# The width-31 convolution accumulates in PSUM instead of SBUF, and two sets of modulation sums start five projections later

## The chip, the cores and the metric

The kernel runs on one core of one Trainium2 chip. The metric is the device time of one execution in microseconds (us); 1197.08 us is the median of three runs of the kernel before (1196.81 to 1198.6). Engines are named as in the profile: PE is TensorE, DVE is VectorE, ACT is ScalarE, POOL is GpSimd, SP issues the transfers.

## The reference

One layer of a diffusion backbone on 1024 latent tokens of width 1024, with 256 context tokens. All data are fp32.

```python
mx = split(silu(c) @ w_ada + b_ada, 6)          # shift, scale, gate of the mixer; the same of the FFN
h  = rms_norm(x, g0) * (1 + mx[1]) + mx[0]
a, gl, q, k, v, o, gates = split(h @ w_in)      # 512 columns each, 16 gate columns
u  = a * sigmoid(gl)
u  = dwconv(u, conv_w, conv_b)                  # 31 taps along each grid row of 64 tokens, per channel
u  = silu(layer_norm(u))
hm = mlstm_bidirectional(q, k, v, gates)        # 4 heads of 128, both directions, start state from the context
m  = sigmoid(o) * head_norm(hm)
x  = x + mx[2] * rms_norm(concat(u, m) @ w_out, g1)
h2 = rms_norm(x, g2) * (1 + mx[4]) + mx[3]
x  = x + mx[5] * rms_norm(conv_ffn(h2), g3)     # up projection, 3-tap convolution, SiLU gate, down projection
```

## The kernel before

Channels lie on the 128 partitions and tokens on the free axis. Every fp32 matmul of a projection is three passes on split operands (a high part and a rest), so each weight block of 128 columns is loaded into a `raw` buffer (three of them), copied to the high part by ACT, and subtracted to the rest by POOL or DVE (line 134).

The order of the first half is this. After the norm of x and its modulation come the first two GLU blocks (column blocks j = 0, 1 of `a` and `gl`) and then j = 2, 3; `glu_evac` (line 274, DVE) writes the product `u[j]`. Then follow the V and gate columns (`vpass(1)`, with the preparation of the context in the middle of it, then `vpass(0)`, with the gate arithmetic `gates()` woven in), and twelve projections in the order k0, q0, k1, k2, k3, q1, q2, q3, o0 to o3 (`proj`, line 679). Into the projections the mLSTM heads are woven: head 0 from the third weave on, then `conv_norm` (the LayerNorm of the convolution), then heads 1 to 3. The output projection (lines 951 to 953) and the FFN follow.

`conv(j)` is the convolution of one block of 128 channels: ACT writes the centre tap and the bias into `accf[:, j]` in SBUF (line 278), and thirty SCALAR_TENSOR_TENSOR instructions on DVE (line 286) add one tap each, with `u[j]` and `accf[:, j]` as inputs, both in SBUF, and `accf[:, j]` as output. Edge taps touch fewer columns: 16 rows of 64 less the offset, so 784 to 1008 elements. All four convolutions are issued at a priority of 100000 behind everything else. A planner orders the instructions of PE, DVE, ACT and POOL at build time by priority and its own estimate of readiness, so taps go into the places where it expects DVE to be free; on the chip each engine then runs its list strictly in order. The SP queue keeps the order of the program.

PSUM has eight banks: pool `mm` with four tiles for projections, pool `tp` with four tiles for everything else (`TP()`): transposes, state updates (`upd`, line 713 on DVE), scores, and the two products of a token chunk in `mlstm_head`, `pv` and `pc`, which four DVE and ACT instructions read (lines 813 to 821).

The modulation vectors are sums over 1024 columns: `ada_step` asks for one more `raw` buffer of `w_ada` (512 KB by SP) and one SCALAR_TENSOR_TENSOR of 128x1024 with an accumulator on DVE (line 228). 32 such steps (shift and scale of the FFN norm, the two gates) are taken two at a time at the start of each of the twelve projections, and the last eight together after them, before the output projection.

Of the kernel before, what the change touches and what calls it, by code (L numbers as in the profile page):

```python
# [8 lines left out]
F32 = mybir.dt.float32  # L9
F32R = mybir.dt.float32r  # L10
AF = mybir.ActivationFunctionType
# [19 lines left out]
def hybrid_block(ctx: ExitStack, tc: tile.TileContext, x, cx, cc, small, gb, w_ada,  # L31
# [10 lines left out]
    wp = wide.enter_context(tc.tile_pool(name="wp", bufs=11, side="right"))  # L42
    rawp = wide.enter_context(tc.tile_pool(name="rawp", bufs=3, side="right"))
    mm = wide.enter_context(tc.tile_pool(name="mm", bufs=4, space=bass.MemoryType.PSUM))
    tp = wide.enter_context(tc.tile_pool(name="tp", bufs=4, space=bass.MemoryType.PSUM))
    early = ExitStack()
    t4 = early.enter_context(tc.tile_pool(name="t4", bufs=10))

# [20 lines left out]
    def wide_tile(n, per, dt=F32):  # L69

        return Cols([S8(dt).rearrange("p (k n) -> p k n", k=per) for _ in range(n // per)])
# [10 lines left out]
    def MM():  # L82
        return mm.tile([P, 512], F32, tag="mm", name="mm")

    def TP():
        return tp.tile([P, 512], F32, tag="tp", name="tp")

    def H2(n=512):
        return sm.tile([P, 512], F32, tag="h2", name="h2", bufs=8)[:, 0:n]
# [185 lines left out]

    def conv(j):
        uv = u[j].rearrange("p (r c) -> p r c", c=W)
        act.activation(out=accf[:, j], in_=u[j], func=AF.Identity, scale=conv_w[:, j, 15:16],
                       bias=conv_b[:, j:j + 1])
        for t in range(CW):  # L280
            o = t - 15
            if o == 0:
                continue
            lo, hi = max(0, -o), min(W, W - o)
            dst = accf[:, j].rearrange("p (r c) -> p r c", c=W)[:, :, lo:hi]
            dve.scalar_tensor_tensor(out=dst, in0=uv[:, :, lo + o:hi + o], scalar=conv_w[:, j, t:t + 1],  # L286
                                     in1=dst, op0=ALU.mult, op1=ALU.add)


    AB2 = const.tile([P, 2, 8], F32, name="AB2")  # L290
# [40 lines left out]
    def ada_step(n):  # L331
        for _ in range(n):
            next(ada_g, None)
# [142 lines left out]
    for j in range(2):  # L476
        u[j] = T4()
        for hf in range(2):
            glu_evac(j, hf, *ps0[j, hf])
    accf = wide_tile(4, 2)  # L480
    vw = None
    with prio(100000):
        conv(0)
# [195 lines left out]
    def proj(i, evac):  # L679
        w = ahead.pop(i)  # L680
        n = order.index(i) + 1
        if n < len(order):
            ahead[order[n]] = load_blk(order[n])
        ada_step(2)
        for hf in range(2):
            hi, lo = hT[hf]
            ps = MM()
            yield from mm_block(ps, w, hi, lo)
            evac(hf, ps)
        return w  # L690
# [53 lines left out]
    def mlstm_head(h):  # L744
# [38 lines left out]
        for g in range(2):  # L783
            hh = H2().rearrange("p (c n) -> p c n", n=P)
            s_ps = TP()
            for t in range(4):
                s = slice((4 * g + t) * P, (4 * g + t + 1) * P)
                pl.matmul(s_ps[:, t * P:(t + 1) * P], kT[h][:, s], qT[:, s], start=True, stop=True)
                yield
            for d in range(2):  # L790
                p = Dt[d][:, g * 512:(g + 1) * 512]
                dve.tensor_tensor(out=p, in0=s_ps, in1=p, op=ALU.mult)
            for t in range(4):
                if t == 2 and pend and hn is not None:
                    yield from tails()
                c = 4 * g + t
                cs = slice(c * P, (c + 1) * P)
                pv, pc = TP(), TP()
                nv = pv[:, 0:258].rearrange("p (d n) -> p d n", d=2)
                nc_ = pc[:, 0:258].rearrange("p (d n) -> p d n", d=2)  # L800
                pl.matmul(pc[:, 0:258], qT[:, cs], Cs[c // 4][:, c % 4].rearrange("p d n -> p (d n)"),
                          start=True, stop=True)
                yield
                for d in range(2):
                    pl.matmul(nv[:, d], Dt[d][:, cs], vx[h][:, c, :], start=True, stop=True)
                    yield
                gc = gcol(0, h, c)
                gs = slice(gc, gc + 63, 62)

                dn = SM(4, "dn")  # L810
                rr, rw = dn[:, 0:2], dn[:, 2:4]
                one = lambda v: v[:, :, 128:129].rearrange("p d o -> p (d o)")
                dve.tensor_tensor(out=rr, in0=one(nc_), in1=wcol[:, gs], op=ALU.mult)
                dve.tensor_tensor(out=rr, in0=one(nv), in1=rr, op=ALU.add)
                dve.scalar_tensor_tensor(out=rw, in0=rr, scalar=-1.0, in1=rr, op0=ALU.mult, op1=ALU.max)
                dve.tensor_tensor(out=rr, in0=rw, in1=thr[:, gs], op=ALU.max)
                dve.reciprocal(out=rr, in_=rr)
                dve.tensor_tensor(out=rw, in0=rr, in1=wcol[:, gs], op=ALU.mult)
                act.mul(out=hh[:, t], in_=nv[:, 0, 0:128], mul=rr[:, 0:1])
                for src, w in ((nv[:, 1], rr[:, 1:2]), (nc_[:, 0], rw[:, 0:1]), (nc_[:, 1], rw[:, 1:2])):  # L820
                    dve.scalar_tensor_tensor(out=hh[:, t], in0=src[:, 0:128], scalar=w, in1=hh[:, t],
                                             op0=ALU.mult, op1=ALU.add)
                dve.bn_stats(out=st[:, c], in_=hh[:, t])
                dve.bn_aggr(out=mv[:, c], in_=st[:, c])
            pend.append((h, g, hh, mv))
# [39 lines left out]
    uf = accf  # L865

    def conv_norm():
        for hf in range(2):
            xh = [T4().rearrange("p (t n) -> p t n", n=512) for _ in range(2)]
            mv = SM(8, "cmv").rearrange("p (t s) -> p t s", s=2)  # L870
            st = SM(24, "cst").rearrange("p (t s) -> p t s", s=6)
            for t in range(4):
                ps = TP()
                tok = slice((4 * hf + t) * P, (4 * hf + t + 1) * P)
                for j in range(4):
                    pl.transpose(ps[:, j * P:(j + 1) * P], uf[:, j, tok], ident)
                    yield
                dve.bn_stats(out=st[:, t], in_=ps)
                dve.bn_aggr(out=mv[:, t], in_=st[:, t])
                rs = SM(1, "crs")  # L880
                rsqrt_pow(rs, mv[:, t, 1:2], 1, "h")
                nb = SM(1, "cnb")
                dve.scalar_tensor_tensor(out=nb, in0=mv[:, t, 0:1], scalar=-1.0, in1=rs, op0=ALU.mult, op1=ALU.mult)
                act.activation(out=xh[t // 2][:, t % 2], in_=ps, func=AF.Identity, scale=rs, bias=nb)
            for j in range(4):
                ps = TP()
                for t in range(4):
                    pl.transpose(ps[:, t * P:(t + 1) * P], xh[t // 2][:, t % 2, j * P:(j + 1) * P], ident)
                    yield
                act.activation(out=uf[:, j, hf * 512:(hf + 1) * 512], in_=ps, func=AF.Silu,  # L890
                               scale=ln_g[:, j:j + 1], bias=ln_b[:, j:j + 1])
        conv_done.append(True)
# [639 lines left out]
```

## Time and profile before

| | |
|---|---|
| median of three runs | 1197.08 us (1196.81 to 1198.6) |
| the profiled execution, own time | 1197.89 us |
| its span, first to last instruction | 1195.8 us |
| PE busy | 1143.2 us (96%) |
| DVE busy | 932.0 us (78%) |
| ACT busy | 523.7 us (44%) |
| POOL busy | 121.3 us (10%) |
| granted clock of TensorE, mean over the span | 0.99 |

Busy time is the union of an engine's instructions. A busy PE includes matmuls that wait inside the pipeline. The mean duration of an instruction reaches from its start to its end; the next one of the same engine may start a little before that end, so a step from start to start is shorter than a duration. Times in a row are from the start of the span.

### The profile page before, as it was taken

Reading aid. Unit: us, or ns where it says so; the run is one execution under the profiler, and the core shown is the slowest. Engines: PE = TensorE matmul, PEld = TensorE weight load, DVE = VectorE, ACT = ScalarE, POOL = GpSimd, SP = SyncE. Lnnn points to the kernel's source line nnn. Section 1 sums busy time; section 2 is a strip of 40 time slices with the busy share of each in tenths; the row PEclk is TensorE's granted clock in tenths of the full one; section 3 lists DMA queues with packets and bytes.
Section 4 is the critical chain, followed back from the end, with each engine's and each line's share of the span. In section 5 each row is a group of like instructions: output and inputs, shape, how many; then the busy total and the mean of one; then the engine's idle time right before and its main releaser. Section 6 shows DMA issues by size and latency. Waiting matters only on the chain.

```text
span 1195.8 us, 14940 instructions
## 1 busy us (share of the span) xinstructions
PE 1143.2 (96%) x5463; PEld 939.5 (79%) x5463; DVE 932.0 (78%) x1702; ACT 523.7 (44%) x952; POOL 121.3 (10%) x106
## 2 busy tenths in 40 slices
PE   6899898999898999999999999999999999999997
PEld 5788787877687777887787888878888878888885
DVE  4899999999779996568966676676668685995585
ACT  6432222242485454357545344343434355454461
POOL 2634120111302210010000000000000000000000
PEclk9899899999999999999999999999999999999999
DMA  8963110442225412442324231323132159633251
GB/s 305 329 207 121 52 37 1 142 147 65 88 89 176 140 56 89 150 167 89 104 73 132 88 122 55 132 89 132 45 132 93 75 192 391 227 112 117 80 220 71
DMA packets 51823, 153.42 MB, mean 128 GB/s; under 512 B 5589, under 2 KB 5925, under 8 KB 49958
## 3 DMA queue, kind: packets, MB, share of 16 engines
q1 hardware_dynamic: 40662, 132.28, 32.0%
q10 hardware_dynamic: 11088, 20.19, 4.5%
q8 instruction: 43, 0.70, 0.2%
q14 instruction: 30, 0.25, 0.1%
HBM read 123.83 MB, written 28.61 MB: 127 GB/s over the span
## 4 chain that ended last, share of the span: by engine, by line
PE 61%; DVE 6%; ACT 1%; issue 1%; POOL 0%; DVEq 0%; POOLq 0%; ACTq 0%
PE mm L1141 8%; PE mm L1143 8%; PE mm L1142 8%; PE c L1369 3%; PE c L1371 3%; PE c L1370 3%; PE tp L1143 3%; PE tp L1142 3%; PE tp L1141 3%; PE a L1369 3%; PE a L1371 3%; PE a L1370 2%; PE mm L951 2%; PE mm L953 2%; PE mm L952 2%; PE tp L508 2%
## 5 line engine op out<-in xcount | busy, mean ns | idle before, releaser
L286 DVE SCALAR_TENSOR_TENSOR s<-t,sml,s 128x864 f32<-128x864 f32 (+14 forms) x120 | 150.5, 1295 | 0.1
L150 PE MATMUL mm<-s,w 128*128 128x512 f32 (+1 forms) x320 | 126.6, 399 | 0.0
L151 PE MATMUL mm<-s,w 128*128 128x512 f32 (+1 forms) x320 | 124.7, 393 | 0.1
L133 ACT ACTIVATE w<-raw 128x1024 fp32r<-128x1024 f32 x94 | 97.0, 1054 | 20.6 <-DMA raw<-in_w_out_dram 5.3
L1141 PE MATMUL mm<-s,w 128*128 128x512 f32 x264 | 104.9, 397 | 0.7 <-ACT h L1214 0.7
L1142 PE MATMUL mm<-s,w 128*128 128x512 f32 x264 | 104.2, 395 | 0.0
L1143 PE MATMUL mm<-s,w 128*128 128x512 f32 x264 | 104.0, 395 | 0.0
L134 DVE TENSOR_TENSOR w<-raw,w 128x1024 fp32r<-128x1024 f32 x77 | 92.3, 1222 | 1.5 <-PE mm L952 0.8
L154 PE MATMUL mm<-s,w 128*128 128x512 f32 (+1 forms) x320 | 93.2, 400 | 0.0
L141 POOL TENSOR_TENSOR r<-yw,mhalf 128x1 f32<-128x1 f32 x16 | 9.7, 608 | 690.7 <-DVE yw L140 690.7
L1141 PE MATMUL mm<-x,w 128*128 128x512 f32 x176 | 70.5, 401 | 0.7 <-ACT h L1205 0.5
L151 PEld LDWEIGHTS mm<-s,w 128*128 128x128 f32 x320 | 60.9, 190 | 11.6 <-POOL s L265 0.7
L1141 PE MATMUL tp<-s,w 128*128 128x512 f32 x176 | 69.5, 395 | 0.0
L150 PEld LDWEIGHTS mm<-s,w 128*128 128x128 f32 x320 | 61.0, 190 | 10.9
L1142 PE MATMUL tp<-s,w 128*128 128x512 f32 x176 | 69.5, 395 | 0.0
L1143 PE MATMUL tp<-s,w 128*128 128x512 f32 x176 | 69.4, 394 | 0.0
L1142 PE MATMUL mm<-x,w 128*128 128x512 f32 x176 | 69.3, 394 | 0.0
L1143 PE MATMUL mm<-x,w 128*128 128x512 f32 x176 | 69.3, 394 | 0.0
L1197 DVE TENSOR_TENSOR h<-mm,h 128x512 f32<-128x512 f32 x22 | 15.2, 692 | 66.3 <-PE mm L1143 66.3
L1271 ACT ACTIVATE s<-x 128x512 fp32r<-128x512 f32 x62 | 38.4, 628 | 64.1 <-PE a L1371 25.0
L1256 DVE TENSOR_TENSOR s<-x,s 128x512 fp32r<-128x512 f32 x62 | 42.8, 695 | 29.0 <-ACT s L1271 29.0
L154 PEld LDWEIGHTS mm<-s,w 128*128 128x128 f32 x320 | 57.0, 189 | 10.2
(311 smaller groups left out, 2916.6 us busy)
## 6 DMA issues: line engine op xcount, KB each, us to landing
raw<-in_w_up_dram SPq DMA_DIRECT2D x44, 512.0 KB, 4.5
zv<-s ACTq DMA_DIRECT2D x77, 256.0 KB, 3.4
raw<-in_w_ada_dram SPq DMA_DIRECT2D x32, 512.0 KB, 4.2
t<-in_w_ada_dram SPq DMA_DIRECT2D x28, 512.0 KB, 5.8
x<-zv SPq DMA_DIRECT2D x14, 1024.0 KB, 5.0
raw<-in_wblk_dram SPq DMA_DIRECT2D x20, 512.0 KB, 4.8
d<-in_w_down_dram SPq DMA_DIRECT2D x28, 256.0 KB, 6.8
x<-zv SPq DMA_DIRECT2D x7, 768.0 KB, 4.2
```

Of the source, the lines that this page charges most:

```text
L133: act.activation(out=hi, in_=raw, func=AF.Copy)
L134: (eng or pool).tensor_tensor(out=lo, in0=raw, in1=hi.bitcast(F32), op=ALU.subtract)
L150: pe.matmul(o, w[0][:, k], hi[:, k], start=(k == 0), stop=False)
L151: pe.matmul(o, w[0][:, k], lo[:, k], start=False, stop=False)
L154: pe.matmul(o, w[1][:, k], hi[:, k], start=False, stop=(k == KT - 1))
L286: dve.scalar_tensor_tensor(out=dst, in0=uv[:, :, lo + o:hi + o], scalar=conv_w[:, j, t:t + 1], in1=dst, op0=ALU.mult, op1=ALU.add)
L1141: pe.matmul(ps, w[0][:, s], b[0][:, k], start=(start and k == 0), stop=False, skip_group_check=True)
L1142: pe.matmul(ps, w[0][:, s], b[1][:, k], start=False, stop=False, skip_group_check=True)
L1143: pe.matmul(ps, w[1][:, s], b[0][:, k], start=False, stop=(k == 3), skip_group_check=True)
L1369: pe.matmul(ps, o[:, 0, s], o[:, 2], start=start, stop=False, skip_group_check=True)
L1370: pe.matmul(ps, o[:, 0, s], o[:, 3], start=False, stop=False, skip_group_check=True)
L1371: pe.matmul(ps, o[:, 1, s], o[:, 2], start=False, stop=stop, skip_group_check=True)
```

## The change

The four-tile pool `tp` shrinks to two tiles, and a new pool `cv` holds one tile of two banks. `conv(j)` takes that tile: DVE writes the centre tap and the bias into it (one TENSOR_SCALAR of 128x1024 in place of the ACT instruction), 29 taps read and write it in PSUM, and the tap of offset 1 comes last and writes its sum into `accf` in SBUF. That tap doesn't reach the last column of a grid row, so one small copy moves these 16 elements.

While convolutions are live (from `conv(0)` to the start of `conv_norm`, in the order of the program) `TP()` has two banks, and `pc` in `mlstm_head` comes from `mm`. Before and after that, every third and fourth call of `TP()` gets one half of the `cv` tile; such a tile is free again when both halves are.

The modulation steps: none at the first five projections, four at each of the last seven, the last four after them.

```diff
-    tp = wide.enter_context(tc.tile_pool(name="tp", bufs=4, space=bass.MemoryType.PSUM))
+    tp = wide.enter_context(tc.tile_pool(name="tp", bufs=2, space=bass.MemoryType.PSUM))
+    cv = wide.enter_context(tc.tile_pool(name="cv", bufs=1, space=bass.MemoryType.PSUM))
...
+    def CV():
+
+        return cv.tile([P, 2, 512], F32, tag="cv", name="cv")
+
+    conv_live = []
+    halves_left = []
+    tp_turn = [0]
+
     def TP():
+
+        if not conv_live:
+            tp_turn[0] += 1
+            if tp_turn[0] % 4 in (3, 0):
+                if not halves_left:
+                    pair = CV()
+                    halves_left.extend((pair[:, 1], pair[:, 0]))
+                return halves_left.pop()
         return tp.tile([P, 512], F32, tag="tp", name="tp")
+
+    def HP():
+        return MM() if conv_live else TP()
...
     def conv(j):
         uv = u[j].rearrange("p (r c) -> p r c", c=W)
-        act.activation(out=accf[:, j], in_=u[j], func=AF.Identity, scale=conv_w[:, j, 15:16],
-                       bias=conv_b[:, j:j + 1])
-        for t in range(CW):
+        pair = CV().rearrange("p h n -> p (h n)")
+        pv = pair.rearrange("p (r c) -> p r c", c=W)
+        fv = accf[:, j].rearrange("p (r c) -> p r c", c=W)
+        dve.tensor_scalar(out=pair, in0=u[j], scalar1=conv_w[:, j, 15:16], scalar2=conv_b[:, j:j + 1], op0=ALU.mult,
+                          op1=ALU.add)
+
+        for t in (*range(15), *range(17, CW), 16):
             o = t - 15
-            if o == 0:
-                continue
             lo, hi = max(0, -o), min(W, W - o)
-            dst = accf[:, j].rearrange("p (r c) -> p r c", c=W)[:, :, lo:hi]
+            dst = (fv if o == 1 else pv)[:, :, lo:hi]
             dve.scalar_tensor_tensor(out=dst, in0=uv[:, :, lo + o:hi + o], scalar=conv_w[:, j, t:t + 1],
-                                     in1=dst, op0=ALU.mult, op1=ALU.add)
+                                     in1=pv[:, :, lo:hi], op0=ALU.mult, op1=ALU.add)
+        dve.tensor_copy(out=fv[:, :, W - 1:W], in_=pv[:, :, W - 1:W])
...
     accf = wide_tile(4, 2)
+    conv_live.append(True)
...
-        ada_step(2)
+        ada_step(4 if n > 5 else 0)
...
-                pv, pc = TP(), TP()
+                pv, pc = TP(), HP()
...
     def conv_norm():
+        conv_live.clear()
```

## Rows read from the trace of the kernel before

**Rows 1.** The page, part 1: busy us (share) x instructions.
```profile
PE 1143.2 (96%) x5463; PEld 939.5 (79%) x5463; DVE 932.0 (78%) x1702; ACT 523.7 (44%) x952; POOL 121.3 (10%) x106
```

**Rows 2.** Stages: length, PE, PEld, DVE, ACT, POOL busy, PEclk, DMA share, GB/s.
```profile
97.00:147.00 50.00, 44.86 (x226) 38.61 (x224) 49.37 (x42) 13.94 (x23) 17.41 (x11) 0.94 0.25 70
147.00:230.00 83.00, 74.52 (x507) 68.17 (x506) 82.63 (x121) 19.50 (x53) 11.19 (x7) 0.96 0.12 41
230.00:308.00 78.00, 71.03 (x385) 59.16 (x383) 77.25 (x157) 23.53 (x61) 15.27 (x5) 1.00 0.34 113
308.00:360.00 52.00, 49.87 (x294) 41.54 (x295) 34.42 (x128) 38.64 (x94) 9.31 (x12) 1.00 0.31 107
360.00:445.00 85.00, 79.33 (x440) 65.58 (x439) 80.29 (x307) 43.13 (x109) 16.17 (x8) 1.00 0.37 121
...
600.00:1195.80 595.80, 586.04 (x2534) 473.84 (x2532) 419.14 (x626) 256.58 (x414) 5.33 (x8) 1.00 0.36 128
```

**Rows 3.** Waits of PE (total us, times, longest): 97 to 147, 230 to 308.
```profile
PE mm L556 <- DVE t L274: 5.1, 2, 3.6
...
PE tp L508 <- DVE h L821: 3.3, 3, 1.5
PE tp L508 <- ACT h L720: 2.4, 1, 2.4
```

**Rows 4.** Groups by line: all taps, then two sizes of tap.
```profile
L286 DVE SCALAR_TENSOR_TENSOR s<-t,sml,s 128x864 f32<-128x864 f32 (+14 forms) x120 | 150.5, 1295 | 0.1
...
L286 DVE SCALAR_TENSOR_TENSOR s<-t,sml,s 128x1008 f32<-128x1008 f32 x8 | 10.0, 1260 | 0.0
...
L286 DVE SCALAR_TENSOR_TENSOR s<-t,sml,s 128x832 f32<-128x832 f32 x8 | 8.6, 1079 | 0.0
```

**Rows 5.** Timeline (start, length, instruction): POOL, then DVE, from 97 us.
```profile
97.60 5.51 POOL L134 TENSOR_TENSOR w<-raw,w 128x1024 fp32r<-128x1024 f32 x2 [16.47 <-ACT w L133]
103.07 7.45 POOL L382 TENSOR_TENSOR w<-raw,w 128x816 fp32r<-128x816 f32 x3
...
97.62 8.97 DVE L286 SCALAR_TENSOR_TENSOR s<-t,sml,s 128x784 f32<-128x784 f32 x3
106.52 0.68 DVE L274 TENSOR_TENSOR t<-mm,h 128x512 f32<-128x512 f32 x1
```

**Rows 6.** Timeline around 346 us: POOL, then DVE.
```profile
346.29 2.38 POOL L134 TENSOR_TENSOR w<-raw,w 128x1024 fp32r<-128x1024 f32 x1 [18.59 <-PE tp L508]
...
345.18 3.35 DVE L713 SCALAR_TENSOR_TENSOR w<-w,dec,tp 128x129 f32<-128x129 f32 x11
```

**Rows 7.** Timeline of DVE, 263 to 268 us.
```profile
263.44 1.02 DVE L286 SCALAR_TENSOR_TENSOR s<-t,sml,s 128x784 f32<-128x784 f32 x1
264.38 0.60 DVE L713 SCALAR_TENSOR_TENSOR w<-w,dec,tp 128x129 f32<-128x129 f32 x2
264.90 1.22 DVE L286 SCALAR_TENSOR_TENSOR s<-t,sml,s 128x976 f32<-128x976 f32 x1
266.05 1.21 DVE L228 SCALAR_TENSOR_TENSOR raw<-raw,G 128x1024 f32<-128x1024 f32 x1
267.20 0.07 DVE L228 DVE_READ_ACCUMULATOR raw<-raw,G 128x1 f32 x1
```

**Rows 8.** Stages, line 228 alone (each sum counts twice, with its accumulator read).
```profile
230.00:308.00 78.00, 13.81 (x24) 1.00 0.34 113
308.00:360.00 52.00, 4.90 (x8) 1.00 0.31 107
360.00:445.00 85.00, 15.84 (x26) 1.00 0.37 121
```

**Rows 9.** Groups by line: a TENSOR_SCALAR of 128x1024 from SBUF to SBUF.
```profile
L1037 DVE TENSOR_SCALAR t<-t,r 128x1024 f32<-128x1024 f32 x8 | 6.0, 753 | 5.7 <-POOL r L141 5.7
```

**Rows 10.** Waits of the SP queue, 200 to 470 us.
```profile
SPq L298 <- DVE raw L228: 9.9, 5, 5.9
```

## The prediction

> **What bounds the kernel now.** The page comes first: PE is busy 96% of the span and DVE 78% [rows 1]. That average hides two kinds of stage, so the table of stages comes next [rows 2]. From 600 us to the end PE works 586.0 of 595.8 us: there only fewer matmuls would help, and the change touches none. From 97 to 308 us it is the other way round: DVE is busy 49.4 of 50, 82.6 of 83 and 77.3 of 78 us, 209.3 of 211 together, while PE leaves 5.1, 8.5 and 7.0 us unused, 20.6 us. [...] The waits of PE say the same: it waits for line 274 (the GLU product, DVE) in the first stretch, and for tp banks that lines 821 (DVE) and 720 (ACT) release in the third [rows 3]. From 308 to 360 us DVE has 17.6 us free; from 360 to 445 us it is busy 80.3 of 85 and PE 79.3: both are close to their limit. PE runs its list in order, so a microsecond that it gains before 308 us arrives at the end unless something gives it back by 445 us.
>
> **The taps in PSUM.** A tap of 1008 elements takes 1260 ns on average and one of 832 takes 1079, a line of 1.03 ns for an element and 223 ns on top; the mean tap has 896 elements and should take 1145 ns. The mean of all 120 is 1295 [rows 4]. The surplus, 150 ns by 120, is 18.0 us, and the timeline shows what it is: while POOL subtracts weight rests back to back from 97.60 to 110.52 us, three taps take 8.97 us in place of about 3. An instruction on the same DVE with one operand in PSUM (line 274) starts inside that stretch and takes its usual 0.68 us [rows 5]. Likewise eleven updates of line 713, with one input in PSUM, take 3.35 us, 0.30 each, through a POOL subtraction of 2.38 us [rows 6]. So a DVE instruction with two SBUF inputs stands still while POOL runs its two-input subtraction, and one with an input in PSUM doesn't. After the change every tap has its accumulator input in PSUM: I take the whole 18.0 us away. Bounds: all of it if nothing else is caught; some returns if the next two-input instruction on DVE (a sum of line 228, a small one of lines 815 and 816) stands still in a tap's stead. In the first stretch, where five taps follow each other, nothing else is there to be caught.
>
> What a tap costs with PSUM as input and output is not in the trace as such. By the nearest rows: a tap of 784 in SBUF steps 0.94 us from start to start, 0.81 for its elements and 0.13 on top; two updates of 129 elements with an input in PSUM step 0.26 each, 0.13 for the elements and 0.13 on top [rows 7]. Reading PSUM costs nothing extra; writing it is not shown. I bound the extra by 0 and by the whole fixed part once more, 0.13 us on each of 120 taps, 15.6 us, and take 0, since the input side is measured and the rate is the same. A shorter step is excluded: both rows give the same fixed part and the same time per element, PSUM or not.
>
> [...]
>
> **The first and last instruction of a convolution.** ACT loses four instructions, which is worth nothing: it is busy 13.9 of 50 us in the first stretch [rows 2]. DVE gains four TENSOR_SCALARs of 128x1024. From SBUF to SBUF that takes 0.75 us [rows 9]; a 1024-element instruction at one element per step starts its successor after 1.15 us, as line 228 does [rows 7]. I take 1.15, as PSUM is involved, and 0.1 for the copy of 16 columns: 4 by 1.25 is 5.0 us (3.4 with the lower bound).
>
> **The modulation sums.** Before, 12 of the 32 run from 230 to 308 us, two earlier, 4 from 308 to 360, 13 from 360 to 445 [rows 8] and one after, at 1.15 us each. The first five projections lose their ten; SP runs ahead of PE, so I expect the eight of the next two projections before 308 us, where 14 were: 6 fewer, 6.9 us off DVE where it is the bound. From 308 to 360 us there are 8 in place of 4: 4.6 us more, hidden in the 17.6 us that DVE has free [rows 2]; without that cover they cost 4.6. From 360 to 445 us there are about 2 more, 2.3 us, and DVE has little room there: I count them in full. Their transfers change in order too: five `raw` buffers per projection pass through three, and SP already waits 9.9 us in five pieces for a buffer that a sum releases [rows 10]. Queued behind such a wait is the weight block of the next projection but one, a whole projection early; I take 0, and the late block is a rival.
>
> **Fewer banks.** From 97 us to the end of head 0 the tp pool has two banks. Two of the context's four groups of transposes must wait for DVE's evacuation; in a stretch that DVE paces this comes out of PE's unused time. In head 0, from 230 to 308 us, PE waits 5.7 us for tp banks with four of them [rows 3]. With half the banks I double that and put the increase on the path: 5.7 us (0 if DVE's lighter list releases them sooner, more in the rival). After 308 us the four banks are back but two come free only together; I take 2 us up to 445 us, between nothing and the 5.7 us of head 0. In the loading stage and the FFN the pairing is hidden: the FFN holds one or two such tiles at a time under matmuls that fill PE [rows 2].
>
> **The sum.** DVE's list up to 308 us shortens by 18.0 + 6.9 - 5.0 = 19.9 us, which PE can follow (27 us). Less 5.7 for banks, 14.2; less 2.3 and 2.0 after 308 us, 9.9 us. The profiled execution took 1197.9 us, 2.1 of them outside the span, which don't change: 1188.0. It lies 0.8 above the median of the runs, so the forecast is 1187.2 us, and its own range 1180 to 1193.
>
> **The rivals.**
> *The banks decide, and it gets slower.* Place: head 0. If each of its 14 state updates and 8 token chunks waits one more instruction of 1.15 us for a bank (a tap or a sum between it and the instruction that releases it), PE loses 25.3 us in place of 5.7. 14.2 becomes -5.4, with the 4.3 us later 9.7 us slower: 1206.8. It decides from 15.6 us of additional bank waits on. For it: two of the three longest waits of that stage are for tp already [rows 3]. Against it: a DVE with less to do releases banks earlier, and `pc` is moved to mm.
> *A tap in PSUM is longer.* At half the bound (0.065 us by 120) 7.8 us go: 1195.0; at the full bound, 15.6, the time is 1202.8. [...] For it: no row shows DVE writing PSUM. Against it: the equal steps of [rows 7].
> *The gain is given back.* DVE from 360 to 445 us is as full as before [rows 2]; if four sums at a time arrive there in a bunch ahead of a head's short instructions, 7 more microseconds (6 sums) are lost: 1194.2.
> *A weight block comes late.* If SP, behind four buffers, delivers three of the last seven blocks 4 us late, 12 us go: 1199.2. For it: the wait in [rows 10]. Against it: none of the waits of PE in [rows 3] is for a weight block, at two steps per projection.
> *The change does nothing.* Taps still stand still behind POOL if the chip looks only at whether some input lies in SBUF. Then 18.0 us stay: 1205.2. [Rows 6] speak against it.
>
> **How the numbers follow.** What a measurement of this kernel can tell from no change is about 0.2%, 2.4 us. Chances: forecast 0.53 (0.51 faster, 0.02 the same); banks 0.13 (slower); longer tap 0.15 (0.06 faster, 0.06 the same, 0.03 slower); given back 0.11 (0.07 faster, 0.04 same); late block 0.05 and no effect 0.03 (together 0.06 slower, 0.02 same). Faster 0.51 + 0.06 + 0.07 = 0.64; slower 0.13 + 0.03 + 0.06 = 0.22; the same 0.14. The range starts where all 19.9 us arrive and nothing is lost (1177), and ends at 1203, which takes in the full bound of the tap and leaves out the two rivals above it, with some tails.
>
> **What would show it.** Right: the mean of line 286 falls from 1295 to about 1150 ns with no tap above 1.4 us; the first stage of taps ends 8 us sooner, PE's waits for line 274 vanish, and the clock of 0.94 rises; the last tap ends near 288 us. Wrong: a tap's step grows by 0.06 us or more (PSUM write); waits for tp from 150 to 290 us grow beyond 15 us (banks); DVE idles in that stage, so that the last tap ends after 300 us; waits of PE for a split weight after 300 us (late blocks).

## The result

The changed kernel takes 1294.26 us (median of 4 runs, 1290.64 to 1296.46); the kernel before took 1197.05 us beside it. The ratio is 1.0806 (95% interval 1.0776 to 1.0836): 97.2 us slower, where 10 us faster was forecast and 1203 was the end of the range. The profiled execution has a span of 1294.7 us at a granted clock of 0.95.

### The profile page after: what moved, and what is told of

Its sections match the earlier page's. It is cut to its first block, busy times and chain, and to the rows that moved or that the text cites. A ratio compares the mean times of both kernels' runs of the same rounds, so it can differ in the third digit from the quotient of the medians.

```text
span 1294.7 us, 14880 instructions
## 1 busy us (share of the span) xinstructions
PE 1164.5 (90%) x5463; PEld 952.4 (74%) x5463; DVE 947.3 (73%) x1710; ACT 521.6 (40%) x948; POOL 114.7 (9%) x106
## 4 chain that ended last, share of the span: by engine, by line
PE 58%; DVE 10%; DMA 4%; ACT 2%; issue 1%; POOL 1%; DVEq 0%; POOLq 0%; ACTq 0%
PE mm L1166 7%; PE mm L1168 7%; PE mm L1167 7%; PE c L1395 3%; PE c L1394 3%; PE c L1396 3%; DMA raw<-in_w_ada_dram 3%; PE a L1395 2%; PE a L1396 2%; PE a L1394 2%; PE mm L978 2%; PE mm L977 2%; PE mm L976 2%; PE cv L532 2%; DVE raw L248 1%; PE tp L1167 1%
## 5 line engine op out<-in xcount | busy, mean ns | idle before, releaser
L308 DVE SCALAR_TENSOR_TENSOR cv<-t,sml,cv 128x784 f32<-128x784 f32 (+14 forms) x116 | 133.3, 1150 | 3.2
L170 PE MATMUL mm<-s,w 128*128 128x512 f32 (+1 forms) x320 | 131.4, 414 | 0.2 <-ACT h L879 0.2
L171 PE MATMUL mm<-s,w 128*128 128x512 f32 (+1 forms) x320 | 128.0, 403 | 0.8 <-POOL s L285 0.6
L153 ACT ACTIVATE w<-raw 128x1024 fp32r<-128x1024 f32 x94 | 97.0, 1054 | 12.0 <-DMA raw<-in_wblk_dram 2.5
L582 PE MATMUL mm<-w,s 128*128 128x272 f32 (+1 forms) x160 | 47.5, 299 | 58.9 <-DVE s L386 58.9
L154 DVE TENSOR_TENSOR w<-raw,w 128x1024 fp32r<-128x1024 f32 x77 | 92.4, 1222 | 2.2 <-ACT w L153 1.3
L174 PE MATMUL mm<-s,w 128*128 128x512 f32 (+1 forms) x320 | 88.9, 395 | 0.0
L582 PEld LDWEIGHTS mm<-w,s 128*128 128x128 f32 x160 | 31.9, 200 | 59.2 <-DVE s L386 59.2
L171 PEld LDWEIGHTS mm<-s,w 128*128 128x128 f32 x320 | 62.4, 195 | 12.2 <-POOL s L285 1.6
L170 PEld LDWEIGHTS mm<-s,w 128*128 128x128 f32 x320 | 62.6, 196 | 11.3 <-ACT h L879 0.6
L174 PEld LDWEIGHTS mm<-s,w 128*128 128x128 f32 x320 | 57.1, 188 | 10.9
L1166 PEld LDWEIGHTS mm<-s,w 128*128 128x128 f32 x264 | 49.9, 189 | 12.7 <-ACT h L1239 1.1
```

The costliest lines, as they stand in the source:

```text
L153: act.activation(out=hi, in_=raw, func=AF.Copy)
L154: (eng or pool).tensor_tensor(out=lo, in0=raw, in1=hi.bitcast(F32), op=ALU.subtract)
L170: pe.matmul(o, w[0][:, k], hi[:, k], start=(k == 0), stop=False)
L171: pe.matmul(o, w[0][:, k], lo[:, k], start=False, stop=False)
L174: pe.matmul(o, w[1][:, k], hi[:, k], start=False, stop=(k == KT - 1))
L582: pe.matmul(o, lo[:, k], w[0], start=False, stop=(k == KT - 1))
```

## The profile after

Page of the changed kernel, parts 1 and 2 (one digit is 32.4 us):

```profile
PE 1164.5 (90%) x5463; PEld 952.4 (74%) x5463; DVE 947.3 (73%) x1710; ACT 521.6 (40%) x948; POOL 114.7 (9%) x106
...
PE   6999710999899868899999999999999999999997
...
PEclk9999865999999987899999999999999999999999
```

PE has a hole at 160 us and thin places between 420 and 550 us, with the clock below full level at both. The stages (columns as in [rows 2]):

```profile
97.00:147.00 50.00, 48.03 (x268) 41.67 (x267) 49.04 (x49) 9.49 (x21) 12.07 (x10) 1.00 0.26 80
147.00:160.00 13.00, 5.75 (x31) 5.56 (x30) 11.35 (x19) 0.44 (x2) 0.00 (x0) 0.63 0.00 0
160.00:225.00 65.00, 6.93 (x51) 6.49 (x49) 62.14 (x58) 2.96 (x8) 0.00 (x0) 0.58 0.00 0
225.00:300.00 75.00, 73.08 (x468) 66.40 (x469) 51.27 (x83) 26.68 (x73) 12.27 (x8) 0.95 0.15 50
300.00:390.00 90.00, 80.97 (x443) 65.88 (x442) 53.07 (x175) 31.71 (x61) 17.85 (x14) 0.96 0.26 83
390.00:520.00 130.00, 110.13 (x539) 89.36 (x537) 100.06 (x331) 59.51 (x161) 15.07 (x8) 0.88 0.41 134
```

The first stage did what was forecast: 268 matmuls in 50 us where there were 226 [rows 2], at full clock. From 160 to 225 us PE runs 51 matmuls. Its waits from 97 to 300 us:

```profile
PE mm L582 <- DVE s L386: 58.9, 1, 58.9
PE tp L376 <- DVE h L381: 7.2, 1, 7.2
```

L582 is a matmul of the V columns, L386 the subtraction that makes the low part of the context tokens (line 363 before). DVE's timeline shows what stands ahead of L386 (L308 are the taps, L381 evacuates the context's transposes):

```profile
158.47 0.99 DVE L381 TENSOR_SCALAR h<-tp,AB 128x256 f32<-128x256 f32 x2 [0.76 <-PE tp L376]
...
167.34 20.41 DVE L308 SCALAR_TENSOR_TENSOR cv<-t,sml,cv 128x976 f32<-128x976 f32 x17
...
190.56 34.41 DVE L308 SCALAR_TENSOR_TENSOR cv<-t,sml,cv 128x784 f32<-128x784 f32 x29
225.00 1.26 DVE L308 SCALAR_TENSOR_TENSOR s<-t,sml,cv 128x1008 f32<-128x1008 f32 x1
226.18 2.49 DVE L386 TENSOR_TENSOR s<-h,s 128x512 fp32r<-128x512 f32 x4
```

The rows to read are the last two: the four subtractions come right after a tap with output `s` (SBUF), the last one of `conv(2)`. ACT had made their other operand at 168.6 us. In the kernel before, the four ran between 161 and 166 us.

The taps by size, all of them, and the new centre tap (L301):

```profile
L308 DVE SCALAR_TENSOR_TENSOR cv<-t,sml,cv 128x784 f32<-128x784 f32 (+14 forms) x116 | 133.3, 1150 | 3.2
...
L308 DVE SCALAR_TENSOR_TENSOR cv<-t,sml,cv 128x832 f32<-128x832 f32 x8 | 8.7, 1087 | 0.2
...
L301 DVE TENSOR_SCALAR cv<-t,sml 128x1024 f32<-128x1024 f32 x4 | 5.4, 1348 | 0.1
...
L308 DVE SCALAR_TENSOR_TENSOR cv<-t,sml,cv 128x1008 f32<-128x1008 f32 x4 | 5.1, 1273 | 0.1
...
L308 DVE SCALAR_TENSOR_TENSOR s<-t,sml,cv 128x1008 f32<-128x1008 f32 x4 | 5.1, 1265 | 0.1
```

No tap stands still any more: the mean is 1150 ns (1295 in [rows 4]), the longest of the 120 takes 1.27 us, and taps of 832 and 1008 elements into PSUM take 1087 and 1273 ns (1079 and 1260 in SBUF).

From 390 to 650 us the longest wait of PE is for the paired tile `cv`, until an instruction of line 845 (821 before) sets it free:

```profile
PE cv L532 <- DVE h L845: 15.7, 6, 8.6
```

## The experiments

Each time is a median with its ratio to the kernel before, timed beside it (1196.6 to 1198.8 us), and the 95% interval of the ratio. Milestones (the end of the V columns, the last tap, the end of the output projection) are starts of the last instruction, in us after the first matmul, which comes about 3 us into the span; times in a profile's rows and stages are from the start of the span. 18 kernels were tried, on three questions.

### The hole: which tile comes late

`accf` and the context's two tiles come from one pool, in the order in which the program asks for them. Before, ACT's centre taps were the first to write `accf`, early. Now its second tile is first written by the last tap of `conv(2)`, and the idea is that the context's tile, asked for later, has to wait for that write. *touch* only brings the first write forward:

```diff
     accf = wide_tile(4, 2)
+    for j in (0, 2):
+        pool.memset(accf[:, j, 0:1], 0.0)
```

> The changed kernel with two one-column writes of accf by POOL ahead of the first convolution, so that both accf tiles exist before the context's tiles are asked for; nothing is left out. Theory (the context's subtractions on DVE stand behind the third convolution because their tile is given out only after accf's second tile, whose first write is now that convolution's last tap): PE's wait of 58.9 us goes, the V columns end about 60 us earlier, 1234 us (1225 to 1242). Rival (DVE's list is late there for another reason, the two banks or the priority of the taps): the wait moves or stays, 1275 us or more.

Measured: 1241.1 us, 1.0371 (1.0355 to 1.0386), inside the range expected by the theory; 53.2 us are back. The wait of 58.9 us is gone, and DVE's timeline has the subtractions behind the evacuations again:

```profile
155.22 0.68 DVE L386 TENSOR_TENSOR s<-h,s 128x512 fp32r<-128x512 f32 x1
156.28 0.68 DVE L386 TENSOR_TENSOR s<-h,s 128x512 fp32r<-128x512 f32 x1
159.34 0.69 DVE L386 TENSOR_TENSOR s<-h,s 128x512 fp32r<-128x512 f32 x1 [0.91 <-ACT s L385]
160.03 0.68 DVE L386 TENSOR_TENSOR s<-h,s 128x512 fp32r<-128x512 f32 x1
```

The V columns now end at 196.9 (205.7 before): the gain that was forecast for the first stage of taps is there. It is lost later: the output projection ends at 574.9 (533.4 before).

### The sums and the shared pair

*ada_only* is the kernel before with the sums moved (`ada_step(4 if n > 5 else 0)`); *touch_ada2* and *free2_ada2* (below) are *touch* and *free2* with the sums where they were (`ada_step(2)`).

> The kernel before with the modulation sums alone moved (none at the first five projections, four at each of the last seven). Theory A (the sums in bunches wait for their transfers on DVE, which runs in order, and hold up heads 1 to 3): 15 to 30 us slower than before, 1212 to 1227 us, with waits of DVE for the transfers of w_ada of 10 us or more. Rival B (the sums are harmless, the banks given out in pairs cost the time after conv_norm): within 5 us of before.

> The kernel of the first run here with the sums two at a time at every projection, as before: the convolution in PSUM and the banks alone, with the tiles in order. Theory A: 1195 to 1212 us. Theory B: 1225 to 1240 us, near the first run. If the convolution in PSUM gives the 14 us that the prediction counted up to the end of the convolution, the LayerNorm of the convolution starts 10 to 15 us earlier than before.

Measured: *ada_only* 1205.5, 1.0068 (1.0053 to 1.0083); *touch_ada2* 1245.0, 1.0402 (1.0384 to 1.0421); *free2_ada2* 1218.5, 1.0175 (1.0158 to 1.0192). The sums alone cost 8 us, about half of the least that theory A expected, and more than the rival's 5. With the convolution in PSUM their move gains 3.9 us (*touch* against *touch_ada2*, which lies above both of its expectations) and 0.8 us (*free2* against *free2_ada2*, within the intervals). They are no main cause.

*ada_only* shows one thing more. Eight sums start there by 308 us where 14 did before, as the prediction counted, and the last tap starts at 276.1 in place of 303.9. Yet PE runs no further from 208 to 308 us (*ada_only* first, then the kernel before; columns as in [rows 2]):

```profile
208.00:308.00 100.00, 92.32 (x485) 76.76 (x485) 97.09 (x201) 29.99 (x74) 17.66 (x8) 0.96 0.28 90
```

```profile
208.00:308.00 100.00, 92.50 (x485) 76.74 (x485) 98.95 (x195) 28.89 (x71) 17.93 (x6) 0.98 0.32 106
```

Six sums fewer on DVE, and taps that are done 28 us sooner, gave PE no matmul more by 308 us, although DVE had been busy nearly all of that stage.

*pairs_only* is the kernel before, SBUF convolution and sums included, with `tp` of two and the paired tile for every third and fourth call; *alt_only* uses the same fixed turns with single tiles:

```diff
-    tp = wide.enter_context(tc.tile_pool(name="tp", bufs=4, space=bass.MemoryType.PSUM))
+    tp = wide.enter_context(tc.tile_pool(name="tp", bufs=2, space=bass.MemoryType.PSUM))
+    tpb = wide.enter_context(tc.tile_pool(name="tpb", bufs=2, space=bass.MemoryType.PSUM))
...
+    tp_turn = [0]
+
     def TP():
+        tp_turn[0] += 1
+        if tp_turn[0] % 4 in (3, 0):
+            return tpb.tile([P, 512], F32, tag="tpb", name="tpb")
```

> The kernel before with the banks alone changed: two tp tiles and a tile of two banks whose halves go to every third and fourth call, through the whole kernel; convolution in SBUF and sums as before. Theory B (halves that come free together cost heads 1 to 3): 15 to 30 us slower, 1212 to 1227 us, with waits of PE for cv banks of 10 us or more. Rival A: within 5 us of before.

> The kernel before with its four tp tiles as two pools of two single tiles, taken in fixed turns (calls 1 and 2 from the one, 3 and 4 from the other), without pairing; all else as before. Pairing theory: within 8 us of before, 1190 to 1206 us, where the run with pairs took 1248. Rival (fixed turn): 1225 us or more.

Measured: *pairs_only* 1248.1, 1.0425 (1.041 to 1.0441), 51 us where 15 to 30 was expected; *alt_only* 1203.5, 1.005 (1.0032 to 1.0069). The fixed turns cost 6 us, the tie between two halves 45, each through the whole kernel. The stage from the end of `conv_norm` to the last projection, *pairs_only* first, then the kernel before (columns as in [rows 2]):

```profile
345.00:474.00 129.00, 106.11 (x543) 85.00 (x542) 101.19 (x332) 68.81 (x179) 14.73 (x8) 0.91 0.34 115
```

```profile
329.00:435.00 106.00, 102.08 (x578) 85.37 (x577) 92.35 (x336) 64.90 (x176) 17.20 (x8) 1.00 0.38 125
```

Fewer matmuls in 23 us more: PE idles 22.9 us instead of 3.9, and the clock averages 0.91 instead of 1.00. The low level that the traces of the kernel before and of the changed one show is 0.50 (from 141 to 147 us in the first, from 180 to 225 us in the second); at that level it would be some 23 us (twice 0.09 of 129), an estimate from these numbers.

*free2* takes the pair away at the place where it hurts: *touch*, with the `cv` tile given up at the start of `conv_norm` and its banks made into two single tiles.

```diff
             tp_turn[0] += 1
+            if tp2 and tp_turn[0] % 4 in (3, 0):
+                return tp2[0].tile([P, 512], F32, tag="tp2", name="tp2")
...
     def conv_norm():
         conv_live.clear()
+        cvs.close()
+        tp2.append(wide.enter_context(tc.tile_pool(name="tp2", bufs=2, ...)))
```

> The first run here (early writes of accf) with the two-bank tile given back at the start of conv_norm and its banks taken up as two single tiles, so that every third and fourth call gets a tile that comes free by itself. Theory (the pairing of the halves costs heads 1 to 3): of the 1241 us some 30 go, 1205 to 1217 us, and PE reaches the output projection 25 to 30 us sooner than there. Rival (the fixed turn, two calls here and two there, costs it, paired or not): 1232 us or more.

> The first run of this call with the sums two at a time at every projection. The sums moved alone cost the kernel before 8 us, in the paired kernel they saved 4. If the pairing theory holds: 1205 to 1217 us; against the first run of this call it tells what the moved sums are worth once the banks are free: between 8 us less and 4 us more.

Measured: *free2* 1217.7, 1.0169 (1.0154 to 1.0185); 23.4 us of *touch* were the pair. Two variants of it: *free4* (one pool of four instead of two and two) 1219.6, 1.0188 (1.0172 to 1.0204), and *free4_ctx* (also two of the context's four transpose groups in `mm`) 1215.95, 1.0161 (1.0144 to 1.0178). *free4* is no faster than *free2*, so the fixed turns cost nothing from `conv_norm` on. *free4_ctx* removes the 7.2 us wait of PE for L381 and ends the V columns at 192.7, yet only 3.6 us arrive.

> All four convolutions in PSUM, accf written early, sums moved as in the change; at the start of conv_norm the two-tile pool and the two-bank tile are both given back and one pool of four single tiles takes their banks, free in any order. If the fixed turn costs what it cost the kernel before alone (6 us): 1209 to 1214 us against 1217.7 for the two pools of two. If the turn is harmless once the banks are single: 1216 to 1220. What is then left over the kernel before is the price of two banks up to conv_norm and of the moved sums.

> The first run of this call with the last two of the context's four groups of transposes in mm tiles in place of tp ones. [...]

### The last 20 us

Three kernels give the banks back earlier, with fewer convolutions in PSUM: *two_psum* (`conv` 0 and 1 in PSUM, banks back before `vpass(0)`), *two_psum4* (the same with one pool of four from there on), *one_psum4* (`conv(0)` alone, pool of four from the context on). The other convolutions stay in SBUF, the sums where they were. `conv_sbuf` is the convolution of the kernel before; the last hunk is that of *two_psum*.

```diff
     accf = wide_tile(4, 2)
+    for j in (0, 2):
+        pool.memset(accf[:, j, 0:1], 0.0)
...
-            conv(j)
+            conv_sbuf(j)
...
+    conv_live.clear()
+    cvs.close()
+    tp2.append(wide.enter_context(tc.tile_pool(name="tp2", bufs=2, ...)))
```

> Convolutions 0 and 1 alone in PSUM, 2 and 3 in SBUF as before; the two banks come back as two single tiles ahead of the second V pass, so that head 0 has four tp banks; sums as before. If the 9 us that the V columns ended sooner with taps in PSUM are kept where head 0 isn't short of banks: 1185 to 1193 us. If the fixed turn or the order of the list costs more: 1200 us or more.

> Convolutions 0 and 1 in PSUM, 2 and 3 in SBUF, sums as before, one pool of four single tiles from the second V pass on. Against 1203.9 us with two pools of two: 1196 to 1200 us if the fixed turn costs some 6 us there too, 1202 or more if it doesn't. Under 1195 it would beat the kernel before.

> Convolution 0 alone in PSUM (its first taps are the five that stood still from 97 to 110 us), the others in SBUF, sums as before; one pool of four single tiles from the context's preparation on, so that nothing after it is short of banks. If the 8 us saved there reach the end: 1188 to 1192 us. If the head stages are paced by something else and give it back, or PE waits at the context for the end of convolution 0: 1196 us or more.

Measured: 1203.9, 1.0057 (1.0042 to 1.0072); 1217.25, 1.0171 (1.0155 to 1.0186); 1198.5, 1.0013 (1.0003 to 1.0023). None is faster than the kernel before. With four, two and one convolutions in PSUM (*free2_ada2*, *two_psum*, *one_psum4*) the time falls towards that kernel; *two_psum4* doesn't fit that line, it was expected near *two_psum* or a little below and is 13 us slower. A long wait of PE in each (the longest in the last two) is for the banks to come back, behind DVE's last write of a convolution (L327) or behind the gates (L644):

```profile
PE tp L551 <- DVE s L327: 6.7, 1, 6.7
```

```profile
PE tp L551 <- DVE ccol L644: 11.2, 1, 11.2
```

```profile
PE tp L393 <- DVE s L327: 11.9, 1, 11.9
```

Then three kernels without any accumulation in PSUM. *sbuf_two* is *free2_ada2* with the SBUF convolution: two banks stand empty. *sbuf_two_pc* takes `pc` from `tp` as well (`HP()` returns `TP()`). *four_pcmm* is the kernel before with `pc` from `mm`.

> The free2_ada2 kernel with the convolution of the kernel before: accumulation in SBUF, the centre tap by ACT, while tp still has two banks from the V columns to conv_norm and pc comes from mm there (the two idle banks hold nothing). Theory A, the two banks cost the 20 us that remain: 1215 to 1228 us, the last tap 10 or more us later than in the kernel before, since DVE idles in head 0 and the held taps are back. Theory B, the accumulation in PSUM or the place of its tiles costs them: 1196 to 1206 us, the last tap near 304 us after the first matmul as before.

> As sbuf_two, but pc comes from the two banks of tp as well, so that a token chunk takes both. If the banks of tp are what head 0 waits for, this is 5 to 15 us slower than sbuf_two; if the cost in sbuf_two comes from pc, which takes banks of mm away from the projections, it is 3 or more us faster.

> The kernel before with one edit: pc comes from mm while convolutions are live; tp keeps its four banks. Theory A (two banks of tp cost the time): within 3 us of the kernel before, 1194 to 1200 us. Rival (pc in mm stalls the projections): 1204 us or more.

Measured: *sbuf_two* 1215.73, 1.0158 (1.0143 to 1.0174), as theory A says, though its last tap is only 6.7 us late (310.6), not 10; *sbuf_two_pc* 1224.28, 1.0233 (1.0218 to 1.0248), 8.5 us more; *four_pcmm* 1202.52, 1.0052 (1.0035 to 1.0068), 6 us, between the two expectations. So the missing banks cost 19 us with nothing accumulated in them. That price takes in `pc` in `mm`, which saves 8.5 us here (without it the price is 27.6), and the fixed turns. But *free2_ada2*, with the same banks and the taps in PSUM, is no faster than *sbuf_two*. That was the open question: where did the held time go?

*three_psum* and *three_sbuf* take one bank from each pool (three and three while the convolution runs, single tiles before and after) and differ in the convolution alone; the first has *touch*'s two memsets.

```diff
-    mm = wide.enter_context(tc.tile_pool(name="mm", bufs=4, space=bass.MemoryType.PSUM))
-    tp = wide.enter_context(tc.tile_pool(name="tp", bufs=4, space=bass.MemoryType.PSUM))
+    mm = wide.enter_context(tc.tile_pool(name="mm", bufs=3, space=bass.MemoryType.PSUM))
+    tp = wide.enter_context(tc.tile_pool(name="tp", bufs=3, space=bass.MemoryType.PSUM))
+    extra = [ext.enter_context(tc.tile_pool(name="e0", bufs=1, space=bass.MemoryType.PSUM))]
...
     accf = wide_tile(4, 2)
+    ext.close()
+    extra.clear()
+    cvp.append(cvs.enter_context(tc.tile_pool(name="cv", bufs=1, ...)))
...
     def conv_norm():
+        cvs.close()
+        extra.append(wide.enter_context(tc.tile_pool(name="e1", bufs=1, ...)))
```

> The kernel before with the convolution of the changed kernel; its two banks come from one tile of mm and one of tp between accf and conv_norm (three and three are left), which are single tiles in fixed turns before and after; accf is first written at the convolution's start; the sums are not moved. Theory A (the held taps are worth their 17 us wherever VectorE doesn't wait for banks): 8 to 17 us faster than three_sbuf, in the best case below the kernel before, 1188 to 1200 us. Rival (VectorE is not what limits head 0 once any bank is missing): within 4 us of three_sbuf.

> As three_psum, with the convolution in SBUF as in the kernel before; two banks stay empty while it runs. This is the price of one bank less for each pool: 1200 to 1212 us by both theories; below 1200 if neither pool needs its fourth bank there.

Measured: *three_psum* 1212.66, 1.0117 (1.0102 to 1.0133); *three_sbuf* 1204.93, 1.005 (1.0033 to 1.0067). One bank from each pool costs 6.2 us (*three_sbuf*), a third of what two of `tp` cost. Both theories on the accumulation missed: PSUM is 7.7 us slower. DVE's time from 85 us up to and with the last tap, added up from the trace (each instruction to the start of the next at most, in us):

| | three_sbuf | three_psum | three_act |
|---|---|---|---|
| 120 taps | 146.3 | 132.3 | 132.5 |
| four centre taps on DVE | 0 | 5.4 | 0 |
| sums (19 in each) | 21.7 | 28.3 | 27.4 |
| all other instructions | 44.9 | 49.2 | 46.4 |
| DVE idle | 5.8 | 11.5 | 11.1 |
| end of V columns / last tap | 207.7 / 303.7 | 197.6 / 311.2 | 190.8 / 301.8 |

Of 14.0 us that the taps lose, the centre taps take 5.4 and the sums 6.6; head 0, which starts 10 us earlier, puts most of 4.3 us of other instructions more ahead of the last tap, and DVE idles 5.7 us more. Four sums of *three_psum* are long: two near 92 us (3.37 and 2.77 us) and two in head 0, under POOL's next weight subtractions (POOL first, then DVE; L148 splits a weight, L242 is a sum):

```profile
217.86 2.40 POOL L148 TENSOR_TENSOR w<-raw,w 128x1024 fp32r<-128x1024 f32 x1 [15.94 <-ACT w L147]
225.04 2.43 POOL L148 TENSOR_TENSOR w<-raw,w 128x1024 fp32r<-128x1024 f32 x1 [4.79 <-ACT w L147]
...
218.21 3.12 DVE L242 SCALAR_TENSOR_TENSOR raw<-raw,G 128x1024 f32<-128x1024 f32 x1
...
226.55 2.00 DVE L242 SCALAR_TENSOR_TENSOR raw<-raw,G 128x1024 f32<-128x1024 f32 x1
```

How sums came under POOL at 92 us is seen in ACT's list. The kernel before, ACT (its POOL and DVE are in [rows 5]):

```profile
95.33 1.24 ACT L278 ACTIVATE s<-t,sml 128x1024 f32<-128x1024 f32 x1 [6.71 <-DVE t L274]
96.48 1.05 ACT L133 ACTIVATE w<-raw 128x1024 fp32r<-128x1024 f32 x1
```

The changed kernel: ACT, then POOL, then DVE (L153 and L154 split a weight, L248 is a sum).

```profile
91.82 1.06 ACT L153 ACTIVATE w<-raw 128x1024 fp32r<-128x1024 f32 x1 [2.34 <-DMA raw<-in_wblk_dram]
...
92.96 6.26 POOL L154 TENSOR_TENSOR w<-raw,w 128x1024 fp32r<-128x1024 f32 x2 [10.59 <-ACT w L153]
...
92.41 1.21 DVE L248 SCALAR_TENSOR_TENSOR t<-t,t 128x1024 f32<-128x1024 f32 x1
...
93.55 3.42 DVE L248 SCALAR_TENSOR_TENSOR t<-t,t 128x1024 f32<-128x1024 f32 x1
...
97.50 2.81 DVE L248 SCALAR_TENSOR_TENSOR t<-t,t 128x1024 f32<-128x1024 f32 x1
```

Before, ACT's list had a centre tap ahead of the weight copy; ACT waited 6.7 us for the GLU product there, so POOL's subtraction started at 97.60 and held taps. Without the centre tap the copy runs 4.7 us earlier, POOL starts at 92.96, and it holds two sums: 3.42 and 2.81 us in place of 1.21. *three_act* gives the centre taps back to ACT, now writing PSUM:

```diff
-        dve.tensor_scalar(out=pair, in0=u[j], ...)
+        act.activation(out=pair, in_=u[j], func=AF.Identity, scale=conv_w[:, j, 15:16], bias=conv_b[:, j:j + 1])
```

> three_psum with the centre tap written into the two PSUM banks by ScalarE (ACT) in place of VectorE. Theory A (the instruction moved to VectorE and what its leaving ScalarE does to the order are what eats the held time): the 5.4 us of the four TENSOR_SCALARs leave DVE, and at least one of the two long sums (3.4 and 2.8 us) is back at 1.2: the last tap ends near 302 to 306 us after the first matmul and the time is 1200 to 1207 us, 5 to 12 below three_psum. Rival (the order of the taps in head 0, with sixteen of them left at 292 us, decides): the last tap stays after 308 us and the time within 3 us of three_psum.

Measured: 1205.17, 1.0068 (1.0051 to 1.0084), 7.5 us below *three_psum* (1.0117), as theory A says. The last tap starts at 301.8 us. One of the two long sums near 92 us is short again:

```profile
92.55 3.35 DVE L242 SCALAR_TENSOR_TENSOR t<-t,t 128x1024 f32<-128x1024 f32 x1
...
96.44 1.21 DVE L242 SCALAR_TENSOR_TENSOR t<-t,t 128x1024 f32<-128x1024 f32 x1
```

The two in head 0 stay long (3.05 and 2.83 us), so the sums still take 5.7 us more than in *three_sbuf*. *three_act* only draws level with *three_sbuf*, although its V columns end 17 us earlier. Why a lead at 190 to 200 us doesn't reach the end may be seen in *free2* against the kernel before, from 330 to 434 us:

```profile
330.00:434.00 104.00, 91.36 (x483) 75.61 (x482) 87.59 (x299) 61.03 (x162) 15.14 (x7) 0.94 0.46 147
```

```profile
330.00:434.00 104.00, 100.08 (x567) 83.65 (x566) 90.38 (x328) 63.90 (x175) 17.20 (x8) 1.00 0.38 124
```

When `conv_norm` begins (306 us after the first matmul in both, right behind the last tap), PE of *free2* has issued 411 of the 672 projection matmuls that follow the V columns, against 365; the heads stand nearly at the same point (126 and 121 of their 543 matmuls). Heads 1 to 3 then have less projection work to run under, and PE of *free2* waits from 330 to 540 us for L851 and L862, lines 821 and 832 of the kernel before:

```profile
PE tp L538 <- DVE h L851: 8.5, 7, 2.2
PE tp L538 <- DVE h L862: 5.8, 3, 3.8
```

From 330 to 434 us there are 84 matmuls fewer and a clock of 0.94. The counts and waits are shown; that this order of PE's list is the reason was not tried, and the count alone doesn't measure the loss: *three_act* has issued 408 at that point and is 7 us slower than the kernel before, *sbuf_two* 343 (7 us later) and is 19 us slower.

## Why the prediction was wrong

The sum, step by step:

- **The taps in PSUM** was right in mechanism and size: 1150 ns against the forecast 1145, no tap held (the longest takes 1.27 us), and taps of 832 and 1008 elements 8 and 13 ns longer with PSUM as output, where the full bound was 130. The rivals "a tap in PSUM is longer" and "does nothing" fall.
- **"Which PE can follow (27 us)"** is 20.6 us of idle PE [rows 2] and, for the rest, the author's estimate of what the low clock costs, which no run shows as such. What the trace of the kernel before shows is a clock of 0.50 from 141 to 147 us, with matmuls of 272 columns (L556 to L558) 0.227 us apart, and 0.126 us apart from 148 to 150 us at a clock of 1.00. From 97 to 147 us PE of the changed kernel ran 42 matmuls more, at 1.00 instead of 0.94.
- **The held time** went partly elsewhere. The bound "some returns if the next two-input instruction stands still" was named and then set to zero for the first stretch, since "nothing else is there to be caught", and the whole 18.0 us were counted. POOL moved 4.6 us forward, to where sums were; in *three_psum* the sums took back 6.6 of 14.0 us, 3.7 of them near 92 us. The four long sums (3.37, 2.77, 3.12 and 2.00 us in place of 1.21) have two SBUF inputs, like the held taps of [rows 5], and lie under POOL's subtractions like them.
- **"ACT loses four instructions, which is worth nothing"** is the step that failed most. Those instructions did three things besides work: they were the first to write `accf`, and without them the context's low part waited for 53 taps and PE for 58.9 us (53 us in the time); they held ACT, and with it POOL, until the taps ran (without them two sums near 92 us lose 3.7 us in *three_psum*); and DVE took over 5.4 us, with the copies 5.8 (5.0 forecast for both). *three_act*, which gives the centre taps back to ACT, is 7.5 us faster than *three_psum*.
- **Fewer banks** was mis-sized: 5.7 us for head 0 and 2 us for the pairs. Measured: 19 us for the two banks with `pc` in `mm` and the fixed turns (*sbuf_two*), 23 us for the pair from `conv_norm` on in the changed kernel (45 for the tie through the whole kernel before). The forecast took the waits of one stage and doubled them; the pair's price fell later, in heads 1 to 3, as idle PE and a lower clock (*touch* from 334 to 460 us: 25.6 us idle at 0.89; *free2* from 334 to 445 us: 12.6 us idle at 0.94; the kernel before from 334 to 435 us: 3.9 us idle at 1.00). The FFN didn't hide all of it either: from the end of the output projection to the last instruction *touch* takes 661.3 us and *free2* 658.3.
- **The modulation sums** were a small term, as forecast: 6.9 us gained and 2.3 lost in the sum, 4.6 net; measured are 0.8 to 3.9 us gained with the convolution in PSUM, but 8 us lost in the kernel before. The late weight block did not show: PE of the changed kernel waits for no split weight from 290 to 640 us.
- **"A microsecond that PE gains before 308 us arrives at the end unless something gives it back by 445 us"** names the condition that failed: V columns 9 us ahead in *touch*, heads 1 to 3 and the output projection later than before. And that DVE is the bound up to 308 us, read from its busy share, held for the first stage, but head 0 doesn't bear it out: *ada_only* took six sums off DVE without one matmul more on PE by 308 us. That the taps, work of the lowest priority, only filled DVE's free places there is a likely reason that was not tried apart. The signs named for the first stage came (268 matmuls, clock 1.00); the last tap near 288 us did not: 303.4 in *touch*, and "DVE idles in that stage" was the sign given for wrong.

The shares, in the order in which the steps were undone: 53.2 (late slot, *touch*) + 23.4 (pair, *free2*) + 19.1 (two banks, `pc` in `mm`, fixed turns, *sbuf_two*), together 95.7 of 97.2 us. The accumulation in PSUM with its centre tap on DVE and the moved sums make up the rest, 1.5 us: nothing gained. Another order would give other shares, since the pair costs more in the kernel before. Of the rivals, "the banks decide" was on the right side, at a tenth of the size and in the wrong place (head 0). No kernel tried was faster than the one before; *one_psum4*, at 1.0013, comes nearest.

## What to carry to other kernels

An instruction that is moved to another engine also leaves a place: ask which tile it was the first to write (that decides when later tiles of its pool get their slot), and what it kept waiting behind it on its old engine. Before accumulating in spare banks, price the banks in the stage that uses them last, and price a lifetime shared by two short-lived halves (45 us here). Held time is only gained if nothing else stands where the holding instruction moves to (in *three_psum* the sums took back 6.6 of 14.0 us). And an engine that is kept busy by filler of the lowest priority need not be the one that sets the pace: ask what the other engine waits for.

## What the runs showed of the hardware

DVE accumulated in PSUM nearly at the pace of SBUF: a tap of 832 elements took 1087 ns with accumulator and output in PSUM (the changed kernel) and 1079 before, one of 1008 elements 1273 and 1260. ACT wrote a centre tap of 128x1024 into two PSUM banks in 1210 ns (*three_act*), into SBUF in 1243 (the kernel before). TensorE's clock in the changed kernel averaged 0.58 between 160 and 225 us, with PE busy 6.9 of 65 us: it was 1.00 from 165 to 170 us, 0.50 from 180 to 225 us, without a matmul, and still 0.50 from 225 to 232 us, with PE busy 5.1 of 7 us. Over the next stage, with PE busy 73.1 of 75 us, it averaged 0.95. A small instruction with two SBUF inputs was long under POOL as well: the changed kernel's 128x8 TENSOR_TENSOR of line 256 took 1.32 us at 100.84 us, under POOL's subtractions that start at 99.19 us, and 0.16 us in the kernel before, where POOL's start at 97.60 us, just after it.
